# Pairs of experts in the first 16 blocks of a MoE layer: 4-byte matmuls in place of hi/lo parts, and one-hot matrices built a step ahead

## The chip, the core and the metric

The kernel runs on one core of a Trainium2 chip. The metric is device time of one launch in microseconds. The kernel before took 1333.95 us (median of 3 runs, 1331.36 to 1334.15).

## What is computed

One transformer layer over 512 latent and 256 context tokens (gated MLP with a tiny attention, neighbourhood attention, merge), then a mixture of 64 experts, 8 per token, and a shared expert. The change lies in the mixture and in the tables that route tokens to it. Cut to that:

```python
scores = sigmoid(h @ w_router)
_, idx = top_k(scores + b_router, 8)
wts = take(scores, idx) / sum * 2.5
# tokens are grouped by expert; each block holds rows of one expert
yb = (silu(h[tok] @ w_gate[e]) * (h[tok] @ w_up[e])) @ w_down[e] * wt
out[tok] += yb                       # for every expert e
```

The model width is 1024, an expert's inner width 256; everything is float32.

## The kernel before, in words

Up to some 600 us the kernel does the mixers, the router and the shared expert's first half. Then `experts` runs 50 blocks of 128 token rows. `ORDER` sets their order: four single experts (blocks 0 to 3), three pairs (4 to 6), two singles (7, 8), one extra block `x` (9) that takes the overflow rows of the experts of blocks 7 and 8 as a pair, then twelve times "pair, single, single", and four singles. A pair holds two experts of 64 rows each. Among the first 16 blocks there are six of length two: 4, 5, 6, 9, 10 and 13.

A block needs the experts' weights: per expert three tiles of 1 MB (two halves of gate and up, one of down), loaded by SP's queue into 13 slots (`pump`, `load_part`); a load is issued when a slot's last reader is done, and at most 4 (`DQ`) are under way. `drop` marks a slot free at its place in the program. The order of loads is: gate/up of the next block, then down of this one.

Tokens are gathered from DRAM by POOL (`fetch`, L1339), transposed on PE (`xpose`, L1351) and split by ACT and DVE into hi and lo parts of type fp32r (`split`, L99, L100). Weights are split the same way, by quarters of 128x1024 (`prep`): a cast on ACT (L1244) and a subtraction on DVE (L1246; on POOL for the quarters numbered in `PQ`). `prep` runs three quarters (`LQ`) ahead of the matmuls. `mm` (L1260) then multiplies: for a single six 128x512 matmuls a quarter. For a pair the stationary operand holds the hi tokens of one expert in one half and the lo tokens of the other in the other half, so that four matmuls a quarter and expert, 32 a block, give each product in two halves of PSUM, which `combine` (L1273 on ACT, L1274 on DVE) adds into an SBUF tile of the `y` buffers. `act` makes silu(gate)*up, `ph` transposes it, `py` (L1304) multiplies by the down weights, unsplit in 4-byte form (for a pair two 64-column matmuls side by side), scales, and scatters with add into one of two DRAM accumulators (L1326), in turn.

`tables` makes, in the background (`bg`, one piece after each quarter-step as long as fewer than `TBN` tables wait), the row lists of each block: a one-hot matrix `oh` on DVE, which compares slot numbers `iot` with the token's position `posm` (L1158 in an interleaved order of rows, L1163 for rows past the capacity), and small matmuls with `vals` (L1168). PE and SP follow the program's order there (`manual_schedule`); DVE, ACT and POOL are ordered by the scheduler. Six pieces of the shared expert's down product (three token blocks, two halves) are put in from block 5 on (`MS`), one a step.

Of the kernel before, what the change touches and what calls it, by code (L numbers as in the profile page):

```python
# [7 lines left out]
F32 = mybir.dt.float32  # L8
# [9 lines left out]
P = 128  # L18
# [51 lines left out]

def bcast(ap, n, off=0):
    return bass.AP(tensor=ap.tensor, offset=ap.offset + off, ap=[[0, P], [1, n]])


class Kern:
# [9 lines left out]
    SLOTS = [0, 1, 2, 3, 8, 9, 5, 7, 4, 6, 10, 11]  # L85

# [979 lines left out]
    def rank(self):  # L1066

        nc, mid, cst, tri, mb = self.nc, self.mid, self.cst, self.tri, self.mb
# [9 lines left out]
        nc.vector.tensor_tensor(krow, pc[:, :NE], cst[:, RC_A:RC_A + NE], op=ALU.mult)  # L1078
        nc.vector.tensor_tensor(krow, krow, cst[:, RC_C:RC_C + NE], op=ALU.add)
# [7 lines left out]
        nc.vector.tensor_scalar(self.perm, cst[:, RC_S:RC_S + P], sm[:, 2:3], None, op0=ALU.is_equal)  # L1087
        nc.tensor.matmul(po, lhsT=cst[:NE, RC_E:RC_E + P], rhs=self.perm[:NE, :NE], start=True, stop=True)
# [56 lines left out]
    def tables(self, blocks, posm, vals, ps=None):  # L1145
# [6 lines left out]
        for i, block in enumerate(blocks):  # L1152
            oh = pool.tile([P, 4, P], BF, name="oh", tag=tag, bufs=2)
            m = P // len(block)
            for p0, (r, t0, cap) in zip((0, m), block):

                k = cap // NQ
                nc.vector.tensor_tensor(oh[:, :, p0:p0 + cap].rearrange("p b (q i) -> p b q i", q=NQ),  # L1158
                                        self.iot[:, None, t0:t0 + cap].rearrange("p b (i q) -> p b q i", q=NQ)
                                        .to_broadcast([P, 4, NQ, k]),  # L1160
                                        posm[:, :, r:r + 1, None].to_broadcast([P, 4, NQ, k]), op=ALU.is_equal)
                if cap < m:
                    nc.vector.tensor_tensor(oh[:, :, p0 + cap:p0 + m],  # L1163
                                            self.iot[:, None, t0 + cap:t0 + m].to_broadcast([P, 4, m - cap]),
                                            posm[:, :, r:r + 1].to_broadcast([P, 4, m - cap]), op=ALU.is_equal)
# [4 lines left out]
            yield  # L1170
# [66 lines left out]
    def prep(self, st, i):  # L1237

        nc = self.nc
        j, q = st.parts[i]  # L1240
# [22 lines left out]
    def combine(self, st, i):  # L1263

        nc = self.nc
        j, q = st.parts[i]
        if st.n == 1 or q < 3:
# [11 lines left out]
    def act(self, st):  # L1279
        nc, p2 = self.nc, self.p2  # L1280
        pg = st.pg[0] if st.n == 1 else st.pgs
# [61 lines left out]
    def xpose(self, st, q):  # L1343
# [9 lines left out]
        self.split(hi, lo, tp.rearrange("p (k s t) -> p k s t", k=4, s=2))  # L1353

    def step(self, es=(), **kw):
        n = max(len(es), 1)
        st = SimpleNamespace(es=es, n=n, parts=[(j, q) for j in range(n) for q in range(4)], gq={}, pg={}, x=None, xg=None,
                             y=None, w=None, h=None, last=False, one=False, room=None, gu=[self.gu_of(e) for e in es], d=lambda i: self.raw[es[i], 2][1])
        st.__dict__.update(kw)
        for e in es:  # L1360
# [13 lines left out]
    def experts(self):  # L1374
# [9 lines left out]
        steps = [self.step([r for r, _, _ in block], block=block) for block in BLOCKS]  # L1384

        parts = lambda st, ns: [(e, n) for e in st.es for n in ns]
# [128 lines left out]
    def extra_block(self):  # L1515
# [10 lines left out]
        nc.vector.tensor_scalar(sm[:, 0, :], sm[:, 0, :], -4097.0, None, op0=ALU.add)  # L1526
        nc.vector.tensor_tensor(oh, self.iot[:, None, :P].to_broadcast([P, 4, P]),
# [14 lines left out]
        nc.vector.tensor_scalar(ex[:, 5:6], ex[:, 4:5], -4096.0, None, op0=ALU.add)  # L1542
        nc.vector.scalar_tensor_tensor(lt, self.iot[:, :NE], ex[:, 5:6], self.order, op0=ALU.is_equal, op1=ALU.mult,
# [60 lines left out]
def prep(inputs):  # L1604
# [61 lines left out]
    a["iota"] = np.broadcast_to(np.arange(2 * P, dtype=np.float32) - 4096, (P, 2 * P))  # L1666
    cst = np.zeros((P, RC_N), np.float32)
    cst[:, 0:12:3] = ar[:, None]
# [3 lines left out]
    cst[:, RC_A:RC_A + NE] = np.where(e < NS, 0, 64)  # L1672
    cst[:, RC_C:RC_C + NE] = np.where(e < NS, 1e6 - e, -e)
    cst[:, RC_K] = np.tile(cst[0, RC_A:RC_A + NE], 2)
    cst[:, RC_K + 1] = np.tile(cst[0, RC_C:RC_C + NE], 2)
    cst[:, RC_K + 2] = np.repeat([0, NE], NE)
    cst[:, RC_S:RC_S + P] = SEQ + [r + NE for r in SEQ]
    cst[:, RC_E:RC_E + P] = ar[:, None] % NE
# [3 lines left out]
    a["cst"] = cst  # L1682
# [27 lines left out]
```

## Time and profile before

| | |
|---|---|
| median of 3 runs | 1333.95 us |
| profiled execution | 1330.07 us, its span 1328.3 us |
| PE busy | 1199.6 us (90%) |
| DVE busy | 924.2 us (70%) |
| ACT busy | 666.6 us (50%) |
| POOL busy | 413.8 us (31%) |
| DMA | 353.36 MB, mean 266 GB/s |
| chain that ended last | DMA 25%, PE 10%, issue 9%, DVE 7% |

Busy times are of one profiled execution. PE's busy time counts matmuls whose ends are modelled and which overlap, so it is not a share of peak. The chain is followed back from the last instruction. The DMA share is the mean busy share of 16 DMA engines; it can read a little over 1.

### The profile page before, as it was taken

Reading aid. Unit: us, or ns where it says so; the run is one execution under the profiler, and the core shown is the slowest. Engines: PE = TensorE matmul, PEld = TensorE weight load, DVE = VectorE, ACT = ScalarE, POOL = GpSimd, SP = SyncE. Lnnn points to the kernel's source line nnn. Section 1 sums busy time; section 2 is a strip of 40 time slices with the busy share of each in tenths; the row PEclk is TensorE's granted clock in tenths of the full one; section 3 lists DMA queues with packets and bytes.
Section 4 is the critical chain, followed back from the end, with each engine's and each line's share of the span. In section 5 each row is a group of like instructions: output and inputs, shape, how many; then the busy total and the mean of one; then the engine's idle time right before and its main releaser. Section 6 shows DMA issues by size and latency. Waiting matters only on the chain.

```text
span 1328.3 us, 18642 instructions
## 1 busy us (share of the span) xinstructions
PE 1199.6 (90%) x6305; PEld 855.4 (64%) x6305; DVE 924.2 (70%) x1577; ACT 666.6 (50%) x1146; POOL 413.8 (31%) x379
## 2 busy tenths in 40 slices
PE   6999999999999999989787999899887997888991
PEld 4875887887777778876553555556554654655660
DVE  4535366666777767687997878877975976667763
ACT  4411254345655544335453666566564665656651
POOL 2410111701211100134554434444343433443422
PEclk9999999999999999989998999899998998999995
DMA  9999454944755546586789899999999999999994
GB/s 325 336 307 287 143 174 103 230 134 112 164 123 136 136 132 230 187 305 197 250 290 278 285 332 372 357 352 333 331 348 356 351 361 353 371 365 358 371 324 143
DMA packets 107322, 353.36 MB, mean 266 GB/s; under 512 B 13937, under 2 KB 41178, under 8 KB 82266
## 3 DMA queue, kind: packets, MB, share of 16 engines
q1 hardware_dynamic: 82634, 289.99, 61.7%
q0 software_dynamic: 24128, 60.59, 19.4%
q10 hardware_dynamic: 464, 1.59, 0.3%
q8 instruction: 50, 0.82, 0.2%
q14 instruction: 46, 0.38, 0.1%
HBM read 323.12 MB, written 39.53 MB: 273 GB/s over the span
## 4 chain that ended last, share of the span: by engine, by line
DMA 25%; PE 10%; issue 9%; DVE 7%; POOL 3%; ACT 1%; POOLq 0%; SPq 0%; DVEq 0%; ACTq 0%
DMA rw<-in_w_exp_dram 21%; PE py L1304 4%; PE pg L1260 4%; DVE gq L1246 3%; DMA accd<-y,ix 2%; DVE xx L100 1%; DMA xg<-h2d,half 1%; DVE oh L1158 1%; POOL xg L1339 1%; ACT gq L1244 1%; POOL accd L1326 1%; DMA accd<-y,half 1%; POOL accb L1326 1%; POOL y L1317 0%; PE xt L1351 0%
## 5 line engine op out<-in xcount | busy, mean ns | idle before, releaser
L1260 PE MATMUL pg<-gq,xx 128*128 128x512 f32 x1328 | 392.2, 432 | 0.6 <-DVE xx L100 0.5
L1246 DVE TENSOR_TENSOR gq<-rw,gq 128x1024 fp32r<-128x1024 f32 x258 | 326.7, 1278 | 75.2 <-ACT gq L1244 73.9
L1244 ACT CAST gq<-rw 128x1024 fp32r<-128x1024 f32 x264 | 272.9, 1047 | 81.1 <-PE pg L1260 48.5
L1260 PEld LDWEIGHTS pg<-gq,xx 128*128 128x128 f32 x1328 | 244.2, 195 | 90.2 <-issue 39.3
L1304 PE MATMUL py<-rw,hT 128*128 128x512 f32 (+1 forms) x560 | 213.3, 617 | 29.6 <-DMA rw<-in_w_exp_dram 28.4
L1317 POOL TENSOR_TENSOR y<-y,gf 128x512 f32<-128x512 f32 x52 | 84.6, 1626 | 283.7 <-ACT y L1316 283.6
L1304 PEld LDWEIGHTS py<-rw,hT 128*128 128x128 f32 (+1 forms) x560 | 73.7, 169 | 111.1 <-issue 98.8
L99 ACT CAST whi<-raw 128x1024 fp32r<-128x1024 f32 (+1 forms) x60 | 61.3, 1023 | 130.9 <-PE mmp L117 52.3
L100 DVE TENSOR_TENSOR wlo<-raw,whi 128x1024 fp32r<-128x1024 f32 (+1 forms) x60 | 71.3, 1189 | 75.8 <-ACT whi L99 75.8
L116 PE MATMUL mmp<-hhi,whi 128*128 128x512 f32 x256 | 103.8, 406 | 0.0
L118 PE MATMUL mmp<-hhi,wlo 128*128 128x512 f32 x256 | 101.1, 396 | 0.0
L117 PE MATMUL mmp<-hlo,whi 128*128 128x512 f32 x256 | 100.8, 394 | 0.0
L1339 POOL DMA_INDIRECT xg<-h2d,ix x50 | 59.0, 1180 | 82.8 <-PE xt L1351 50.5
L100 DVE TENSOR_TENSOR xx<-xt,xx 128x512 fp32r<-128x512 f32 x100 | 68.2, 684 | 15.5 <-ACT xx L99 15.1
L99 ACT CAST xx<-xt 128x512 fp32r<-128x512 f32 x100 | 58.3, 584 | 12.4 <-PE xt L1351 11.6
L771 POOL DMA_DIRECT2D q<-qdr x32 | 17.7, 554 | 147.9 <-PE stp L818 143.1
L1351 PE MATMUL xt<-ident,xg 128*128 128x128 f32 x400 | 60.7, 275 | 1.9 <-DMA xg<-h2d,half 1.9
L1326 POOL DMA_INDIRECT accb<-y,ix x31 | 56.0, 1806 | 11.1 <-POOL y L1317 7.4
L1351 PEld LDWEIGHTS xt<-ident,xg 128*128 128x128 f32 x400 | 49.5, 143 | 12.3 <-issue 2.7
L1319 DVE SCALAR_TENSOR_TENSOR y<-py,tw,gf 128x512 f32<-128x512 f32 x52 | 38.8, 745 | 26.0 <-PE py L1304 18.3
L116 PEld LDWEIGHTS mmp<-hhi,whi 128*128 128x128 f32 x256 | 48.2, 188 | 12.5 <-issue 3.0
L118 PEld LDWEIGHTS mmp<-hhi,wlo 128*128 128x128 f32 x256 | 48.1, 188 | 10.6 <-issue 0.8
(422 smaller groups left out, 2162.3 us busy)
## 6 DMA issues: line engine op xcount, KB each, us to landing
rw<-in_w_exp_dram SPq DMA_DIRECT2D x195, 1024.0 KB
raw<-in_w_in_dram SPq DMA_DIRECT2D x40, 512.0 KB
araw<-in_w_ada_dram SPq DMA_DIRECT2D x64, 256.0 KB
araw<-in_w_ada_dram SPq DMA_DIRECT2D x16, 512.0 KB
k<-kdr POOLq DMA_DIRECT2D x32, 192.0 KB, 6.3
nab<-in_nab_dram SPq DMA_DIRECT2D x24, 256.0 KB
x<-in_x_dram SPq DMA_DIRECT2D x8, 512.0 KB
q<-qdr POOLq DMA_DIRECT2D x32, 128.0 KB, 5.1
```

The lines of the kernel that those rows point to most:

```text
L99: self.nc.scalar.copy(hi, src)
L100: (eng or self.nc.vector).tensor_tensor(lo, src, self.r32(hi), op=ALU.subtract)
L116: mm(ps, lhsT=ahi, rhs=bhi, start=first, stop=False)
L117: mm(ps, lhsT=ahi, rhs=blo, start=False, stop=False)
L118: mm(ps, lhsT=alo, rhs=bhi, start=False, stop=last)
L1244: nc.scalar.copy(t[:, 0, :, sl], src)
L1246: eng.tensor_tensor(t[:, 1, :, sl], src, self.r32(t[:, 0, :, sl]), op=ALU.subtract)
L1260: nc.tensor.matmul(pg, lhsT=st.x[:, q * 2 + k, a, :], rhs=t[:, b, k, :], start=q + k + n == 0, stop=q + k + n == 3 + len(terms))
L1304: nc.tensor.matmul(py[s], lhsT=st.hT[:, j, s], rhs=d[:, j * D + c * 512:j * D + c * 512 + 512], start=j == 0, stop=j == 1)
L1317: nc.gpsimd.tensor_tensor(o, o, gf, op=ALU.mult)
L1326: nc.gpsimd.indirect_dma_start(out=to[:], out_offset=bass.IndirectOffsetOnAxis(ap=ix[:cap], axis=0), in_=y, in_offset=None, bounds_check=S ...
L1351: self.nc.tensor.transpose(tp[:, k * P:k * P + P], st.xg[:, (q * 4 + k) * P:(q * 4 + k + 1) * P], self.ident)
```

## The change

For the six blocks of length two among the first `NB` = 16 (`whole`), tokens and weights are not split. `xpose` copies the transposed tokens as they are; `prep` only looks the tiles up; `mm` multiplies 4-byte tokens of each expert (64 columns) with the weight tile itself, the two experts side by side in the halves of PSUM. Such a block has 4 steps of two experts' quarters instead of 8 of one. Its gate/up tiles are dropped after the matmuls that read them, both experts' first halves together, and are loaded in that order. `combine` does nothing and `act` reads PSUM.

In the tables the slot numbers are kept in bfloat16, in the interleaved order already (`SLOTS_OF`, 896 columns, cast by a POOL DMA), so that one comparison without strides makes each expert's part; `posm` gets one more instruction. The `yield` moves up: a block's `oh` is made in one step and its table matmuls run in the next. The constants for `rank` move to a tile of their own in the `u` buffers.

```diff
+    NB = 16
 def place(...):
         nc.vector.scalar_tensor_tensor(posm, mask, -4096.0, pp, op0=ALU.mult, op1=ALU.add)
+        nc.vector.tensor_scalar(posm, posm, 4096.0, None, op0=ALU.add)
 def route_consts(self):
-        self.iot = mid.tile([P, 2 * P], F32, name="iot")
-        nc.sync.dma_start(self.iot, self.A["iota"])
+        self.iot = mid.tile([P, len(SLOTS_OF)], BF, name="iot")
+        nc.gpsimd.dma_start(self.iot, self.A["iota"])
...
+        self.cst2 = self.p1.tile([P, RK_N], F32, name="cst2", tag="u", bufs=2)
+        nc.sync.dma_start(self.cst2, self.A["cst2"])
 def tables(...):
-                k = cap // NQ
-                nc.vector.tensor_tensor(oh[:, :, p0:p0 + cap].rearrange("p b (q i) -> p b q i", q=NQ),
...
-                if cap < m:
...
+                c = TURNS[m, t0, cap]
+                nc.vector.tensor_tensor(oh[:, :, p0:p0 + m], self.iot[:, None, c:c + m].to_broadcast([P, 4, m]),
+                                        posm[:, :, r:r + 1].to_broadcast([P, 4, m]), op=ALU.is_equal)
+
+            yield
             for b in range(4):
...
-            yield
 def prep(self, st, i):
+        if st.whole:
+            q = st.parts[i]
+            st.gq[i] = [st.gu[j](q)[0][0] for j in range(st.n)]
+            return
 def mm(self, st, i):
+        if st.whole:
+            q, m = st.parts[i], P // st.n
+            if q == 0:
+                st.pg[0] = self.ps2.tile([P, 512], F32, name="pg", tag="gu", bufs=2)
+            for k in range(2):
+                for j, t in enumerate(st.gq[i]):
+                    r = slice(j * m, j * m + m)
+                    nc.tensor.matmul(st.pg[0][r], lhsT=self.r32(st.x)[:, q * 2 + k, 0, r], rhs=t[:, k, :],
+                                     start=q + k == 0, stop=q + k == 4)
+            if q % 2:
+                for e in st.es:
+                    self.drop(e, q // 2)
+            return
 def combine(self, st, i):
+        if st.n == 1 or st.whole:
+            return
 def xpose(self, st, q):
-        self.split(hi, lo, tp.rearrange("p (k s t) -> p k s t", k=4, s=2))
+        if st.whole:
+            self.nc.scalar.copy(self.r32(st.x)[:, q * 4:q * 4 + 4, 0, :], tp.rearrange("p (k t) -> p k t", k=4))
+        else:
+            self.split(hi, lo, tp.rearrange("p (k s t) -> p k s t", k=4, s=2))
 def experts(self):
+        steps = [self.step([r for r, _, _ in block], block=block, whole=len(block) > 1 and i < self.NB)
+                 for i, block in enumerate(BLOCKS)]
+        parts = lambda st, ns: [(e, n) for n in ns for e in st.es] if st.whole else [(e, n) for e in st.es for n in ns]
```

On PE, in the second step of block 5 (a pair), the order before was this (`pg` the gate/up product, `xt` the transposed tokens of the next block, `ph` the transposed inner rows and `py` the down product of the block before or of the shared expert, `ptab` a table):

```order
L1260 MATMUL pg<-gq,xx 128x512 x4
L1290 MATMUL ph<-ident,hh 128x128 x2
L1304 MATMUL py<-rw,hT 128x512 x2
L1168 LDWEIGHTS oh
L1168 MATMUL ptab<-vals,oh 128x6
```

And the same step now:

```order
L1281 MATMUL pg<-rw,xx 64x512 x4
L1326 MATMUL ph<-ident,hh 128x128 x2
L1387 MATMUL xt<-ident,xg 128x128 x4
L1340 MATMUL py<-rw,hT 128x512 x2
L1186 LDWEIGHTS oh
L1186 MATMUL ptab<-vals,oh 128x6
```

The step's `pg` covers a quarter of both experts instead of one, so a block has half as many steps, and the next block's transposes come in the first half of the block.

On DVE, the stretch between two blocks' down products inside the pairs read as follows before (`gq` the lo part of a weight quarter, `y<-y,pg` the sum of the halves, `hh` the inner rows):

```order
L1319 SCALAR_TENSOR_TENSOR y<-py,tw,gf 128x512
L1158 TENSOR_TENSOR oh<-iot,posm_6304 128x4x64 x2
L1158 TENSOR_TENSOR oh<-iot,posm_6304 128x512
L1274 TENSOR_TENSOR y<-y,pg 64x512
L1246 TENSOR_TENSOR gq<-rw,gq 128x1024
L1158 TENSOR_TENSOR oh<-iot,posm_6304 128x512
L1158 TENSOR_TENSOR oh<-iot,posm_6304 128x4x64 x2
L1246 TENSOR_TENSOR gq<-rw,gq 128x1024
L100 TENSOR_TENSOR xx<-xt,xx 128x4x128 x2
L1246 TENSOR_TENSOR gq<-rw,gq 128x1024
```

And now:

```order
L1355 SCALAR_TENSOR_TENSOR y<-py,tw,gf 128x512
L1180 TENSOR_TENSOR oh<-iot,posm_6307 128x4x64 x2
L1321 TENSOR_TENSOR hh<-sg,pg 128x256
L1180 TENSOR_TENSOR oh<-iot,posm_6307 128x512
L1350 TENSOR_TENSOR y<-py,gf 128x512
L1180 TENSOR_TENSOR oh<-iot,posm_6307 128x512
L1180 TENSOR_TENSOR oh<-iot,posm_6307 128x4x64 x2
L1355 SCALAR_TENSOR_TENSOR y<-py,tw,gf 128x512
```

The weight and token subtractions and the sums of halves are gone there; one-hot matrices and the output products remain.

## Rows read from the trace of the kernel before

**Rows 1.** The timeline of PE: first gate/up matmuls of block 4 and of block 7.

```profile
672.84 1.18 PE L1260 MATMUL pg<-gq,xx 128*128 128x512 f32 x4
...
746.73 1.64 PE L1260 MATMUL pg<-gq,xx 128*128 128x512 f32 x6
```

**Rows 2.** Stages (from:to, us): PE, PEld, DVE, ACT, POOL busy; PEclk, DMA share, GB/s.

```profile
618.00:672.00 54.00, 45.99 (x241) 32.29 (x240) 52.43 (x80) 27.47 (x42) 34.16 (x19) 0.94 0.77 242
672.00:747.00 75.00, 62.02 (x284) 35.66 (x283) 65.85 (x92) 37.35 (x49) 32.56 (x19) 0.86 0.95 296
747.00:820.00 73.00, 66.99 (x283) 41.61 (x283) 56.52 (x64) 47.95 (x67) 32.33 (x23) 0.98 0.96 328
820.00:950.00 130.00, 119.34 (x561) 76.98 (x560) 107.53 (x151) 82.23 (x112) 59.77 (x38) 0.97 1.01 347
950.00:1250.00 300.00, 258.88 (x1106) 167.29 (x1105) 215.73 (x247) 179.28 (x247) 120.03 (x81) 0.97 1.02 357
```

**Rows 3.** DMA from 618, 672, 820 us: bytes; a queue's share; scatters, us to landing.

```profile
DMA packets 2546, 13.09 MB, mean 242 GB/s; under 512 B 640, under 2 KB 640, under 8 KB 1261
...
DMA packets 3775, 22.21 MB, mean 296 GB/s; under 512 B 595, under 2 KB 595, under 8 KB 1537
q0 software_dynamic: 1267, 3.86, 26.1%
...
accd<-y,rows POOLq DMA_INDIRECT x2, 9.4
...
DMA packets 26096, 152.29 MB, mean 354 GB/s; under 512 B 4827, under 2 KB 4827, under 8 KB 10219
```

**Rows 4.** The chain that ended last, in order of time: start, us, what.

```profile
735.49 1.87 PE py L1304 x8
737.36 1.14 PE pg L1260 x4
...
763.07 1.72 PE py L1304 x4
...
773.17 0.92 PE pg L1260 x4
```

**Rows 5.** Groups of instructions, shapes apart: xcount | busy us, mean ns | idle before.

```profile
L1260 PE MATMUL pg<-gq,xx 128*128 128x512 f32 x1328 | 392.2, 432 | 0.6 <-DVE xx L100 0.5
L1246 DVE TENSOR_TENSOR gq<-rw,gq 128x1024 fp32r<-128x1024 f32 x258 | 326.7, 1278 | 75.2 <-ACT gq L1244 73.9
L100 DVE TENSOR_TENSOR xx<-xt,xx 128x512 fp32r<-128x512 f32 x100 | 68.2, 684 | 15.5 <-ACT xx L99 15.1
L1274 DVE TENSOR_TENSOR y<-y,pg 64x512 f32<-64x512 f32 x32 | 21.9, 684 | 14.6 <-ACT y L1273 14.1
L1158 DVE TENSOR_TENSOR oh<-iot,posm 128x512 bf16<-128x512 f32 x13 | 13.2, 1024 | 0.0
L1158 DVE TENSOR_TENSOR oh<-iot,posm 128x256 bf16<-128x256 f32 x16 | 12.6, 817 | 0.0
L1057 DVE SCALAR_TENSOR_TENSOR posm<-sw,pp 128x256 f32<-128x256 f32 x1 | 0.4, 401 | 0.0
```

**Rows 6.** Busy time of instructions on tile oh alone: PE, PEld, DVE, PEclk, DMA share, GB/s.

```profile
618.00:672.00 54.00, 2.86 (x52) 2.18 (x52) 14.22 (x16) 0.94 0.77 242
672.00:747.00 75.00, 4.42 (x80) 3.62 (x80) 22.30 (x31) 0.86 0.95 296
```

**Rows 7.** Timeline of DVE and of POOL: single instructions.

```profile
657.46 0.28 DVE L1158 TENSOR_TENSOR oh<-iot,posm 128x128 bf16<-128x128 f32 x1
...
555.60 0.56 POOL L121 TENSOR_TENSOR sm<-sm,mhalf 128x1 f32<-128x1 f32 x1 [62.41 <-DVE sm L955]
```

**Rows 8.** Waits: of the stage 672 to 747 us, and of the whole span.

```profile
ACT y L1273 <- DMA accd<-y,rows: 7.4, 1, 7.4
ACT y L1316 <- DMA accd<-y,half: 6.9, 1, 6.9
...
PE py L1304 <- DMA rw<-in_w_exp_dram: 28.4, 7, 7.0
```

More of the change, by code (lines that the diff above doesn't have):

```diff
@@ L68, with turns @@
 BLOCKS, SEQ = plan(ORDER)
+def turns():
+    runs, at = [range(NE)], {}
+    n = NE
+    for block in BLOCKS:
+        m = P // len(block)
+        for _, t0, cap in block:
+            if (m, t0, cap) not in at:
+                at[m, t0, cap] = n
+                n += m
+                runs.append([t0 + (p % (cap // NQ) * NQ + p // (cap // NQ) if p < cap else p) for p in range(m)])
+    return at, [t for r in runs for t in r]
+TURNS, SLOTS_OF = turns()
 def bcast(ap, n, off=0):
@@ L1066, in rank @@
     def rank(self):
-        nc, mid, cst, tri, mb = self.nc, self.mid, self.cst, self.tri, self.mb
+        nc, mid, cst, cst2, tri, mb = self.nc, self.mid, self.cst, self.cst2, self.tri, self.mb
         col = lambda i: cst[:, i:i + 1]
@@ L1077, in rank @@
         krow = mid.tile([P, NE], F32, name="krow")
-        nc.vector.tensor_tensor(krow, pc[:, :NE], cst[:, RC_A:RC_A + NE], op=ALU.mult)
-        nc.vector.tensor_tensor(krow, krow, cst[:, RC_C:RC_C + NE], op=ALU.add)
+        nc.vector.tensor_tensor(krow, pc[:, :NE], cst2[:, RK_A:RK_A + NE], op=ALU.mult)
+        nc.vector.tensor_tensor(krow, krow, cst2[:, RK_C:RK_C + NE], op=ALU.add)
         sm = mid.tile([P, 4], F32, name="rsm")
@@ L1086, in rank @@
         self.perm = mid.tile([P, P], F32, name="perm")
-        nc.vector.tensor_scalar(self.perm, cst[:, RC_S:RC_S + P], sm[:, 2:3], None, op0=ALU.is_equal)
-        nc.tensor.matmul(po, lhsT=cst[:NE, RC_E:RC_E + P], rhs=self.perm[:NE, :NE], start=True, stop=True)
+        nc.vector.tensor_scalar(self.perm, cst2[:, RK_S:RK_S + P], sm[:, 2:3], None, op0=ALU.is_equal)
+        nc.tensor.matmul(po, lhsT=cst2[:NE, RK_E:RK_E + P], rhs=self.perm[:NE, :NE], start=True, stop=True)
         self.order = mid.tile([P, NE], F32, name="order")
@@ L1280, in act @@
         nc, p2 = self.nc, self.p2
-        pg = st.pg[0] if st.n == 1 else st.pgs
+        pg = st.pg[0] if st.n == 1 or st.whole else st.pgs
         sg = p2.tile([P, FF], F32, name="sg", tag="sg", bufs=1)
@@ L1358, in step @@
                              y=None, w=None, h=None, last=False, one=False, room=None, gu=[self.gu_of(e) for e in es], d=lambda i: self.raw[es[i], 2][1])
+        st.whole = False
         st.__dict__.update(kw)
+        if st.whole:
+            st.parts = list(range(4))
         for e in es:
@@ L1525, in extra_block @@
         oh = p2.tile([P, 4, P], BF, name="xoh", tag="oh", bufs=2)
-        nc.vector.tensor_scalar(sm[:, 0, :], sm[:, 0, :], -4097.0, None, op0=ALU.add)
-        nc.vector.tensor_tensor(oh, self.iot[:, None, :P].to_broadcast([P, 4, P]),
+        nc.vector.tensor_scalar(sm[:, 0, :], sm[:, 0, :], -1.0, None, op0=ALU.add)
+        c = TURNS[P, 0, P]
+        nc.vector.tensor_tensor(oh, self.iot[:, None, c:c + P].to_broadcast([P, 4, P]),
                                 sm[:, 0, :, None].to_broadcast([P, 4, P]), op=ALU.is_equal)
@@ L1665, in prep @@
     a["tri"] = np.stack([ar[:, None] < ar[None], np.ones((P, P), bool)], 1).astype(np.float32)
-    a["iota"] = np.broadcast_to(np.arange(2 * P, dtype=np.float32) - 4096, (P, 2 * P))
+    a["iota"] = np.broadcast_to(np.array(SLOTS_OF, np.float32), (P, len(SLOTS_OF)))
     cst = np.zeros((P, RC_N), np.float32)
+    cst2 = np.zeros((P, RK_N), np.float32)
     cst[:, 0:12:3] = ar[:, None]
@@ L1671, in prep @@
     e = np.arange(NE)
[L1672 to L1675, printed above, removed]
+    cst2[:, RK_A:RK_A + NE] = np.where(e < NS, 0, 64)
+    cst2[:, RK_C:RK_C + NE] = np.where(e < NS, 1e6 - e, -e)
+    cst[:, RC_K] = np.tile(cst2[0, RK_A:RK_A + NE], 2)
+    cst[:, RC_K + 1] = np.tile(cst2[0, RK_C:RK_C + NE], 2)
     cst[:, RC_K + 2] = np.repeat([0, NE], NE)
-    cst[:, RC_S:RC_S + P] = SEQ + [r + NE for r in SEQ]
-    cst[:, RC_E:RC_E + P] = ar[:, None] % NE
+    cst2[:, RK_S:RK_S + P] = SEQ + [r + NE for r in SEQ]
+    cst2[:, RK_E:RK_E + P] = ar[:, None] % NE
     for block in BLOCKS:
@@ L1681, in prep @@
             cst[:, RC_L + r] = max(cst[0, RC_L + r], t0 + cap)
-    a["cst"] = cst
+    a["cst"], a["cst2"] = cst, cst2
     return {k: np.ascontiguousarray(v) for k, v in a.items()}
```

18 lines of the change are left out of this document (4 added, 14 removed).

## The prediction

> **What bounds the kernel now.** I read the busy times by stage first, then the DMA figures of the stages, the chain, the groups, and the waits. In PE's timeline block 4's first matmul starts at 672.84 us and block 7's at 746.73 [rows 1], which cuts the expert part into stages: A, 618 to 672 us, blocks 0 to 3; B, 672 to 747, the three pairs 4 to 6; C, 747 to 820; and the rest. The reader should look at which column is nearly full in each row of [rows 2].
>
> In A, DVE is busy for 52.4 of 54 us and the DMA for a share of 0.77 only: weight loads wait for slots, and slots for DVE. In B, DVE has 65.9 of 75 us, PE 62.0 at a granted clock of 0.86 of 2.4 GHz (part of the time at 1.2), and the DMA 0.95. In C, PE has 67.0 of 73 us, the DMA 0.96. From 820 us on the DMA stands at 1.01 to 1.02 for 430 us. PE waits for weights there, 28.4 us in all for the down product [rows 8]. So three limits follow each other: DVE, then PE, then the DMA; and whatever the first two lose is lost for good only as far as the DMA idles. The DMA is the bank: once it is full, time gained ahead of it comes through to the end only as DMA work that was done earlier.
>
> I take 1.02, the late stages' share, as full. The DMA work in A, B and C is 54 x 0.77 + 75 x 0.95 + 73 x 0.96 = 41.6 + 71.3 + 70.1 = 183.0 us of share, which takes 179.4 us at 1.02, in place of 202. The most that can be gained by this reckoning is 22.6 us: 13.2 in A, 9.4 in B and C.
>
> **PE.** A pair's 32 gate/up matmuls go in fours of 0.92 us [rows 4], 7.4 us a block. Now there are 16 matmuls of 64 columns, 4-byte, with the experts side by side. The trace has this form already in a pair's down product: eight records, which are four matmuls, in 1.87 us, where a single's four records (two matmuls of 128 columns) take 1.72 [rows 4]. Two halves therefore run together, and 16 matmuls take 4 x 1.87 = 7.5 us: even. One thing is added: four full-width matmuls right behind a 64-column `py` take 1.14 us against 0.92 [rows 4], so a return from half width costs 0.22 us. A whole block returns to full width once a step, 0.9 us a block. The Trainium skill (TensorEngine Tiling (Array Packing), Key Properties) says that changing the tiling mode drains the engine, which speaks against this change; it gives no time, so the sum by the page would only say "more than 7.5", and the row's 0.22 us stands.
>
> **DVE, stage A.** The one-hot instructions there take 14.2 us in 16 records [rows 6]. After the change the same blocks (five pairs, four singles) need 14 comparisons without strides. Such an instruction isn't in the trace; the token subtraction, one pass over 512 elements, takes 684 ns [rows 5]. It can't be slower than today's strided one (1024 ns [rows 5]), and the 128-element one of 0.28 us [rows 7], less than a third of which would be its start, gives about 0.4 us for 512 at the very least. I take 684, which is nearest in form, and 0.41 for 256 elements (between 0.28 and today's 0.82): 4 x 0.68 + 10 x 0.41 = 6.8, so 7.4 us saved (0 to 9). Block 4's first three quarters are prepared in A, one on POOL and two on DVE, 2 x 1.28 = 2.6 us [rows 5]; two token subtractions of 0.68 make 1.4 us. The added instruction on `posm` costs what its neighbour does, 0.4 us [rows 5], and is on the way to the first table. DVE falls by 11.0 to 41.4 us. PE is late next, with 46.0 us busy; of the 8.0 us in which it stands still I keep half, for the making of the first routing tables, which the change leaves as they are. Stage A: 50 instead of 54, **4 us** gained.
>
> **DVE, stage B.** The 24 - 3 = 21 weight subtractions x 1.28 are 26.9 us, six sums of halves x 0.68 4.1, four token subtractions 2.7, and half of the tables' steps go: 22.3 us of one-hot work [rows 6] becomes some 8. DVE falls from 65.9 to 17.9 us. PE is next: its 62.0 us at a clock of 0.86 are 53.3 at full clock; 2.6 come for returns, and half of the tables' 4.4 us [rows 6] goes, 53.7 us of 75. The scatters come close: block 3's one, three shared ones and two each of blocks 4 and 5 go into two accumulators in turn, landing in 9.4 us [rows 3], so five in a row take some 47 us. The stall that they make today through the `y` buffers, 7.4 and 6.9 us on ACT [rows 8], should shrink, since a whole block takes no `y` tile for its sums. So engines could do B in 54 us, and C, with two whole blocks' returns, in 69.
>
> **DMA.** It can't follow that: 141.4 us of share work in B and C need 138.6 us at 1.02, more than the engines' 123. B and C thus take 138.6 in place of 148: **9.4 us** gained. Behind 820 us nothing changes but the start.
>
> **Sum.** 4 + 9.4 = 13.4 us. The profiled execution took 1330.07 us (span 1328.3), 3.9 below the median of 1333.95. 1330.1 - 13.4 = 1316.7 there, 1320.5 as a median; I say 1320.
>
> **What costs nothing, and its cover.** The `iot` load goes to POOL's queue, behind `tri` and ahead of the first `sm`; POOL stands idle for 62.4 us there [rows 7]. Were the cover gone it would be one issue, which I put at the 0.56 us of its neighbour there [rows 7]. On SP `cst2` takes one `u` buffer and the router's weights the next, one `nab` load later; only the loads queued behind could suffer, by the time until the second buffer is free, and three raw buffers stand between them and PE. ACT loses eight casts a pair, which nobody waits for once DVE is out of the way. One POOL subtraction moves from block 4 to block 7.
>
> **The wait that is added.** A slot of a whole block now waits for PE's matmul instead of DVE's subtraction, which ran up to three quarters ahead: on average half a block later. On SP all later loads and the reads of expert numbers queue behind. Against that, when block 4 starts, 6 of 13 slots are held (a shared tile, block 3's down, its own four); the seven others take all of block 5's gate/up, block 4's down and one of block 6. That is a block ahead, with four loads allowed at once, so I cost it at nothing.
>
> **Rivals.**
>
> *Bytes, not shares* (chance 0.22). A share of 0.95 in B moves 296 GB/s, the same core moves 354 in the late stages [rows 2, 3]. If the difference is hidden idling and not the indirect transfers (26.1% of share in B for 3.86 of 22.21 MB [rows 3], which speaks for these), B and C with 46.2 MB need 130 us at 354, a gain of 17.6, with A 21.6: 1312, and to 1305 if A too gets fuller. The Trainium skill (DMA: Bandwidth & Descriptors, Specifications) puts the HBM limit of a core at about 358 GB/s; by it B and C would need 129 us, the same rival. The trace agrees with it: 357 over 300 us [rows 2].
>
> *Slots held too long: slower* (0.14). If the later drop starves the loads, B and C run nearer to A's manner. With 0.90 in B and C they need 141.4/0.90 = 157 us, 9 more than now, less A's 4: 1339. At A's own 0.77 it would be 184 us and the kernel past 1360, which the seven free slots make unlikely. The point that decides is a share of 0.93 over B and C, where A's gain is used up. The row for it is A's 0.77, made by slots.
>
> *No change* (0.13). The halves don't run together when weights are the moving operand and tokens the stationary one, so that the change doesn't do what it says on PE: 16 matmuls x 0.86 = 13.8 us a block instead of 7.5. B then needs 73 us on PE, C (blocks 9 and 10) 81, together 154 against 148, which eats A's 4 us and 2 more: 1336. Against it stands the identical form of `py`. Or the indirect transfers keep their time whatever comes, and only 2 us are won.
>
> **Numbers.** The forecast has 0.51, with 1313 to 1329 as its own range. A measurement can tell about 0.2%, 2.7 us, from no change. Faster by more, below 1331.3: 0.51 + 0.22 = 0.73; within: 0.13; slower: 0.14. The range leaves out the outer part of the bytes rival and most of the slower one: 1306 to 1335.
>
> **What would show it.** On DVE 258 weight subtractions become some 210 and 32 sums of halves 20; 1328 fp32r gate/up matmuls become 1136, with 192 records of the 4-byte form, eight in 1.87 us. One-hot instructions on DVE are 34 + 2 x 16 = 66, a 512-element one near 0.68 us. Block 7's first matmul should come 20 to 28 us earlier if the engines alone decide, and PE should wait for weights from about there, much earlier than now; the DMA share from 670 us on at 1.0 or above. I am wrong in the sum if block 7 starts early but the last weights don't land some 13 us earlier; wrong in the mechanism if the share in B falls below 0.93, or if eight 4-byte records take over 3 us.

## The result, and the profile after

The changed kernel takes 1315.93 us (median of 4 runs, 1313.55 to 1321.14) where the kernel before takes 1334.05 in the same comparison (4 runs, 1331.36 to 1335.59): a ratio of 0.988, 95% interval 0.9856 to 0.9905, 18.1 us less. The profiled execution of the change took 1315.69 us with a span of 1313.8, so the two profiled spans differ by 14.5. That is less than 18.1 because the profiled execution of the kernel before, at 1330.07 us, was 3.9 faster than its median.

PE's timeline, which answers to [rows 1]: the first gate/up matmul of all, of block 4 and of block 7.

```profile
622.54 1.96 PE L1294 MATMUL pg<-gq,xx 128*128 128x512 f32 x6
...
671.50 1.94 PE L1281 MATMUL pg<-rw,xx 128*64 128x512 f32 x8
...
721.65 1.66 PE L1294 MATMUL pg<-gq,xx 128*128 128x512 f32 x6
```

Block 7 starts 25.1 us earlier. Stage A, counted from the first gate/up matmul, now lasts 49.0 us and stage B 50.2, where [rows 1] and the first gate/up matmul at 618.2 give 54.7 and 73.9. The stages again, cut at the new borders, in the columns of [rows 2]:

```profile
618.00:671.00 53.00, 48.68 (x254) 33.52 (x255) 47.12 (x81) 28.18 (x45) 31.88 (x19) 0.97 0.78 246
671.00:721.00 50.00, 49.24 (x246) 18.74 (x245) 18.51 (x34) 13.20 (x22) 21.14 (x15) 1.00 0.98 346
721.00:806.00 85.00, 79.61 (x366) 40.68 (x362) 40.71 (x54) 33.27 (x50) 40.55 (x32) 0.96 1.00 346
806.00:936.00 130.00, 110.98 (x514) 68.73 (x513) 88.83 (x112) 69.63 (x96) 50.28 (x34) 0.93 1.00 341
936.00:1236.00 300.00, 263.62 (x1114) 169.78 (x1113) 214.63 (x247) 182.12 (x251) 121.89 (x84) 0.96 1.02 361
```

In stage B, DVE fell to 18.5 us, PE is busy for 49.2 of 50 at full clock, and the DMA moves 346 GB/s instead of 296. From 671 us on the DMA is as good as full (0.98 and 1.00, where 1.0 or above was forecast), and the engines begin to wait for it: not PE first, as forecast, but ACT's cast, which stands ahead of PE. From 671 to 806 us (in all, times, longest) it waited for weights

```profile
ACT gq L1265 <- DMA rw<-in_w_exp_dram: 13.9, 6, 6.4
```

where the kernel before had 1.3 us of that wait. The groups, columns as in [rows 5]:

```profile
L1294 PE MATMUL pg<-gq,xx 128*128 128x512 f32 x1136 | 331.6, 428 | 0.8 <-DVE gq L1267 0.8
L1267 DVE TENSOR_TENSOR gq<-rw,gq 128x1024 fp32r<-128x1024 f32 x210 | 264.1, 1270 | 82.5 <-ACT gq L1265 81.4 <-issue 0.3
L1281 PE MATMUL pg<-rw,xx 128*64 128x512 f32 x192 | 48.1, 623 | 0.0
L1180 DVE TENSOR_TENSOR oh<-iot,posm 128x512 bf16<-128x512 bf16 x34 | 26.2, 774 | 10.0 <-PE ptab L1186 8.5 <-PE ph L1326 1.4
L1180 DVE TENSOR_TENSOR oh<-iot,posm 128x256 bf16<-128x256 bf16 x32 | 17.5, 578 | 5.8 <-PE ptab L1186 5.8
L1310 DVE TENSOR_TENSOR y<-y,pg 64x512 f32<-64x512 f32 x20 | 13.7, 685 | 9.6 <-ACT y L1309 9.3
```

The counts are those forecast (210, 20, 1136, 192, 34 and 32). An undisturbed 512-element one-hot takes 0.68 to 0.69 us; the mean of 774 ns holds a few that took much longer.

Where the time went is read best from the DMA's bytes between 618 and 820 us. Ahead of 618 the program is nearly the same, and behind 820 the DMA is full in both. First the kernel before, then the change (all traffic; then the weights' queue with its share):

```profile
DMA packets 10671, 59.26 MB, mean 293 GB/s; under 512 B 2111, under 2 KB 2111, under 8 KB 4778
...
q1 hardware_dynamic: 6605, 48.16, 65.5%
```

```profile
DMA packets 11729, 64.33 MB, mean 318 GB/s; under 512 B 2347, under 2 KB 2347, under 8 KB 5422
...
q1 hardware_dynamic: 7072, 51.56, 66.6%
```

The change moves 5.07 MB more in this window, and 5.07 MB at the 354 GB/s of [rows 3] are 14.3 us: the spans differ by 14.5. The weights' share rose by a mere 1.1 points of 202 us, 2.2 us of share, for 3.4 MB more. With POOL's queue, which went from 24.6% to 27.1%, it is 3.6 points or 7.3 us, half of what came. This is the main reading of the case: bytes tell what was banked, the share doesn't.

### The profile page after: what moved, and what is told of

It is laid out like the page before. It is cut to its first block, busy times and chain, and to the rows that moved or that the text cites. A ratio compares the mean times of both kernels' runs of the same rounds, so it can differ in the third digit from the quotient of the medians.

```text
span 1313.8 us, 18428 instructions
## 1 busy us (share of the span) xinstructions
PE 1199.2 (91%) x6305; PEld 835.5 (64%) x6305; DVE 831.2 (63%) x1470; ACT 612.5 (47%) x1086; POOL 397.7 (30%) x380
## 4 chain that ended last, share of the span: by engine, by line
DMA 30%; PE 15%; DVE 5%; issue 3%; ACT 1%; POOL 1%; SPq 0%; POOLq 0%; DVEq 0%; ACTq 0%
DMA rw<-in_w_exp_dram 27%; PE py L1340 5%; PE pg L1294 5%; DVE gq L1267 2%; PE pg L1281 2%; PE xt L1387 1%; DMA accb<-y,rows 1%; DMA xg<-h2d,half 1%; DMA accd<-y,ix 1%; DVE oh L1180 1%; PE mmp L137 1%; DMA accb<-y,ix 1%; ACT gq L1265 1%; PE mmp L136 1%; PE mmp L135 1%
## 5 line engine op out<-in xcount | busy, mean ns | idle before, releaser
L1294 PE MATMUL pg<-gq,xx 128*128 128x512 f32 x1136 | 331.6, 428 | 0.8 <-DVE gq L1267 0.8
L1267 DVE TENSOR_TENSOR gq<-rw,gq 128x1024 fp32r<-128x1024 f32 x210 | 264.1, 1270 | 82.5 <-ACT gq L1265 81.4
L1294 PEld LDWEIGHTS pg<-gq,xx 128*128 128x128 f32 x1136 | 207.0, 192 | 78.7 <-issue 30.2
L1265 ACT CAST gq<-rw 128x1024 fp32r<-128x1024 f32 x216 | 222.0, 1047 | 64.7 <-DMA rw<-in_w_exp_dram 42.1
L1340 PE MATMUL py<-rw,hT 128*128 128x512 f32 (+1 forms) x560 | 216.9, 625 | 37.2 <-DMA rw<-in_w_exp_dram 30.0
L1353 POOL TENSOR_TENSOR y<-y,gf 128x512 f32<-128x512 f32 x52 | 75.1, 1445 | 270.6 <-ACT y L1352 270.5
L119 DVE TENSOR_TENSOR xx<-xt,xx 128x512 fp32r<-128x512 f32 x88 | 60.2, 685 | 30.4 <-ACT xx L118 29.7
L1375 POOL DMA_INDIRECT xg<-h2d,ix x50 | 55.4, 1107 | 76.8 <-PE xt L1387 45.7
L1387 PEld LDWEIGHTS xt<-ident,xg 128*128 128x128 f32 x400 | 49.2, 143 | 20.6 <-issue 13.2
L118 ACT CAST xx<-xt 128x512 fp32r<-128x512 f32 x88 | 51.4, 585 | 16.3 <-PE xt L1387 15.4
```

Of the source, the lines that this page charges most:

```text
L118: self.nc.scalar.copy(hi, src)
L119: (eng or self.nc.vector).tensor_tensor(lo, src, self.r32(hi), op=ALU.subtract)
L1265: nc.scalar.copy(t[:, 0, :, sl], src)
L1267: eng.tensor_tensor(t[:, 1, :, sl], src, self.r32(t[:, 0, :, sl]), op=ALU.subtract)
L1294: nc.tensor.matmul(pg, lhsT=st.x[:, q * 2 + k, a, :], rhs=t[:, b, k, :], start=q + k + n == 0, stop=q + k + n == 3 + len(terms))
L1340: nc.tensor.matmul(py[s], lhsT=st.hT[:, j, s], rhs=d[:, j * D + c * 512:j * D + c * 512 + 512], start=j == 0, stop=j == 1)
```

## Experiments

All are compared with runs of the kernel before on the same chip (ratio and its 95% interval). The table has one profiled execution of each: first gate/up matmul, length of stage A (to block 4's first matmul) and B (to block 7's), from PE's timeline; MB moved from 618 to 820 us; the span; and what the bytes alone would give, 1328.3 - (MB - 59.26)/0.354.

| kernel | ratio | start | A | B | MB | span | by bytes |
|---|---|---|---|---|---|---|---|
| before | 1 | 618.2 | 54.7 | 73.9 | 59.26 | 1328.3 | |
| change | 0.988 (0.9856 to 0.9905) | 622.5 | 49.0 | 50.2 | 64.33 | 1313.8 | 1314.0 |
| change again | 0.988 (0.9847 to 0.9912) | 618.3 | 49.0 | 49.1 | 65.74 | 1309.6 | 1310.0 |
| tables only | 0.9948 (0.9923 to 0.9972) | 622.5 | 53.9 | 70.2 | 59.30 | 1328.1 | 1328.2 |
| 4-byte pairs only | 0.9893 (0.9853 to 0.9933) | 616.9 | 54.4 | 49.0 | 64.37 | 1317.1 | 1313.9 |
| blocks 4 to 6 | 0.9846 (0.9809 to 0.9883) | 619.0 | 49.0 | 49.3 | 66.83 | 1312.0 | 1306.9 |
| all pairs | 0.9813 (0.9777 to 0.9849) | 619.8 | 49.4 | 49.9 | 65.17 | 1308.6 | 1311.6 |
| all pairs again | 0.9843 (0.9812 to 0.9874) | 617.1 | 53.1 | 49.1 | 64.68 | 1309.3 | 1313.0 |
| all but block 9 | 0.9833 (0.9794 to 0.9873) | 622.7 | 53.1 | 50.2 | 63.50 | 1314.1 | 1316.3 |
| halves in turn | 0.9864 (0.9821 to 0.9907) | 620.4 | 53.3 | 49.6 | 63.59 | 1318.9 | 1316.1 |
| work put back | 0.9915 (0.9885 to 0.9945) | 618.9 | 54.0 | 49.1 | 63.29 | 1317.3 | 1316.9 |
| sums in own tile | 0.9913 (0.9885 to 0.9942) | 617.8 | 53.3 | 63.2 | 63.61 | 1319.9 | 1316.0 |
| one half | one run | 618.3 | 49.4 | 50.5 | 65.06 | 1312.5 | 1311.9 |
| same step | 0.9897 (0.9866 to 0.9928) | 621.1 | 51.2 | 49.0 | 64.34 | 1317.9 | 1313.9 |

The last two columns agree within 5.1 us over the 13 profiles, whatever was edited, and for eight of them within 3.0. Reckoned by the DMA's share of the same window instead (all queues, 1.02 as full), all 13 would end later than they do, by 2.4 to 12.3 us.

What the bytes leave over is hardly noise alone. The three kernels with the late pairs in 4-byte form (all pairs twice, all but block 9) end 2.2 to 3.7 us before what the bytes give; of the ten others none ends more than 0.4 us before. Behind 820 us these three move 340.0 to 340.8 GB/s to their end, the others 334.8 to 339.0. So the stretch behind 820 us is not quite the same in every kernel.

**1. The two parts apart.** Tables only: no pair in 4-byte form.

```diff
-    NB = 16
+    NB = 0
```

> The changed kernel with no pair in 4-byte form: one-hot tables without strides, made a step ahead, all else as before. Bank theory (time won ahead of the DMA-bound part comes through as DMA work done earlier): stage A ends some 4 us earlier, and in the pairs the one-hot work falls by 8 to 10 us of a DVE that had 65.9 of 75 us, of which a third to a half counts; in all 4 to 8 us, 1326 to 1330 us. Tables-do-most rival: 14 us or more, 1320 or less. No-value rival (late start again, DVE's time taken by the next wait): within 2.7 us of 1334.

4-byte pairs only: the kernel before with the change's edits to `prep`, `mm`, `combine`, `act`, `xpose`, `step` and the order of loads, and the tables, `iota` and `cst` as they were. Against the changed kernel that is, in the tables:

```diff
-                c = TURNS[m, t0, cap]
-                nc.vector.tensor_tensor(oh[:, :, p0:p0 + m], self.iot[:, None, c:c + m].to_broadcast([P, 4, m]),
-                                        posm[:, :, r:r + 1].to_broadcast([P, 4, m]), op=ALU.is_equal)
-            yield
+                k = cap // NQ
+                nc.vector.tensor_tensor(oh[:, :, p0:p0 + cap].rearrange("p b (q i) -> p b q i", q=NQ),
...
```

> The kernel before with pairs among the first 16 blocks in 4-byte form; one-hot tables with strides and not a step ahead, as before. Bank theory: stage A as before, B shorter by some 20 us on the engines, of which 10 to 14 us reach the end: 1320 to 1324 us. Tables-do-most rival: 1329 or more. If the two parts of the change add, the gains of this kernel and of the tables alone sum to about 18 us; if each alone is enough to fill the DMA queue, their sum is well over 18.

Measured: 1327.88 us and 1320.02 us against 1335.61, so 7.7 and 15.6 less. The sum, 23.3, is over the 18.1 of both, but the intervals (some 3 and 5 us to either side) don't exclude that they add. The 4-byte pairs carry the larger part, and all of the shortening of B (49.0). The tables alone take 3.7 us out of B. Their profiled execution shows nothing of the 7.7 us: it starts at 622.5 us, its A takes 53.9, and its span of 1328.1 is that of the kernel before, so that gain rests on the medians alone. In B the next wait grew in place of the one-hot work; ACT's waits from 672 to 747 us of the tables-only kernel:

```profile
ACT y L1309 <- DMA accd<-y,rows: 12.3, 1, 12.3
```

It was 7.4 us before [rows 8]. The copy that waited starts at 712.78 us, and ACT's next cast of a weight only behind it, at 713.26.

**2. Sums of halves in a tile of their own**, in the tables-only kernel, to test that wait.

```diff
-            st.y = self.y_tile()
-            st.pgs = st.y[:, 512:]
+            st.pgs = self.p2.tile([P, 512], F32, name="pgs", tag="pgs", bufs=1)
...
-        st.h = p2.tile([P, FF], F32, name="hh", tag="hh", bufs=2)
+        st.h = p2.tile([P, FF], F32, name="hh", tag="hh", bufs=1)
```

> The tables alone (no pair in 4-byte form), and the sums of halves in a tile of their own instead of a y buffer, so that no scatter holds them up; hh has one buffer to make room. y-buffer theory (in stage B a two-part pair's sum waits for an earlier scatter, 7.4 us before and 12.3 us with the tables alone, and ACT's casts queue behind it): stage B falls from 74 to 60 to 66 us, and the kernel, 7 us faster with the tables alone, gains 4 to 8 us more: 1319 to 1324 us. Chain rival (what costs is cast, subtraction and product in turn, wherever the sum stands): B stays above 70 us, and the kernel is that of the tables alone, 1325 to 1329.

Measured: 1322.11 us against 1333.12, and B 63.2 us, as the y-buffer theory had it. Its stage B, from block 4 to block 7, and block 7's first matmul:

```profile
671.00:734.00 63.00, 57.15 (x282) 32.57 (x281) 55.90 (x78) 36.51 (x48) 32.14 (x18) 0.95 0.97 333
```

```profile
734.27 1.64 PE L1294 MATMUL pg<-gq,xx 128*128 128x512 f32 x6
```

PE has 57 and DVE 56 of the 63 us, so with the wait gone both are near full. B's 23.7 us thus go by steps: 3.7 by the tables, 7.0 by not waiting for a `y` buffer, and the last 13 only when the pairs need no split (one profile of each). At the end, the ratio goes from 0.9948 to 0.9913; the intervals overlap a little.

**3. The weights' split put back**, without a reader.

```diff
             st.gq[i] = [st.gu[j](q)[0][0] for j in range(st.n)]
+            for src in st.gq[i]:
+                t = self.p2.tile([P, 2, 2, 2 * FF], F32R, name="gq", tag=f"gq{self.ngq % self.GQ}")
+                self.ngq += 1
+                nc.scalar.copy(t[:, 0], src)
+                eng = nc.gpsimd if self.ngq in self.PQ else nc.vector
+                eng.tensor_tensor(t[:, 1], src, self.r32(t[:, 0]), op=ALU.subtract)
             return
```

> The changed kernel with the weight casts (ACT) and subtractions (DVE, POOL) of the 4-byte pairs put back into tiles that nobody reads; sums of halves and token subtractions stay away, tables and PE stay as changed. DVE theory: the 21 subtractions of 1.28 us in stage B bring DVE back to some 45 us and, in turn with ACT's casts, hold slots and the SBUF; if DVE's relief is the gain, stage B returns to 60 to 70 us and the kernel to 1322 to 1328. PE rival (the gain of B is the half-as-many PE steps and PE's clock): B stays near 50 us and the time near 1316. On the DMA: if the weights' bytes per unit of share fall from 391 GB/s towards before's 357 with DVE busy again, the engines' traffic is what made the DMA slower in B; if they stay near 390, the queue's depth is.

Measured: 1321.69 us against 1331.34, between the two forecasts. Its stage B:

```profile
673.00:722.00 49.00, 49.00 (x251) 18.75 (x249) 44.94 (x56) 28.83 (x39) 24.69 (x14) 1.00 0.96 344
```

DVE is busy for 44.9 of 49 us again, and B is no longer for it. So DVE's load alone is not what made B slow. In experiment 2, where the split is still there, PE is busy for 57.2 of 63 us at a clock of 0.95; here it is busy for all 49.0 at 1.00. So of the last 13 us some 6 are waits of PE, which went with its dependence on cast, subtraction and sum, and the rest is PE's own work, which is less in the 4-byte form and at a higher clock. How much is the clock and how much the work, no run took apart. From 671 to 721 us the weights' queue moved 13.80 MB in a share of 0.693, 398 GB/s of share; the 391 of the change did not fall, so DVE's traffic is not what made the DMA slower before. Against the change on the same chip (1316.14 us, experiment 7) the kernel is 5.5 us slower, so the work isn't free. A took 54.0 us in its profile, the longer of two lengths that other kernels show as well, so whether the extra work cost that time is open.

**4. Do two 64-column halves run together?** First the loops swapped, so that one expert's two matmuls of a quarter come before the other's.

```diff
-            for k in range(2):
-                for j, t in enumerate(st.gq[i]):
+            for j, t in enumerate(st.gq[i]):
+                for k in range(2):
```

> The changed kernel with the two loops around the 4-byte matmul swapped, so that one expert's two matmuls of a quarter come before the other's. Pairing theory (two halves of the array run together only when neighbours in the order stand on different halves): eight records take 2.6 to 3.4 us instead of 1.87 to 1.94, a pair's gate/up 10 to 14 us instead of 7.5 to 8, stage B some 8 to 18 us longer on PE, and 5 to 15 us of that reach the end: 1320 to 1331. If the halves run together in whichever order, 1314 to 1318.

Then one half left alone.

```diff
                 for j, t in enumerate(st.gq[i]):
+                    if j and q + k not in (0, 4):
+                        continue
```

> The changed kernel, in which the second expert of a 4-byte pair leaves out its gate/up product except the first and the last of its eight matmuls; so the two middle quarters have two matmuls of 64 columns (four records) with no neighbour on the other half. Half-price theory (a 64-column 4-byte matmul takes half of a 128-column one by itself): four records in 0.9 to 1.0 us. Pairing theory (two halves run at the same time): four records alone take as long as eight together, 1.7 to 1.9 us.

Measured: swapped, 1314.89 us against 1331.34, B 49.6; eight records still take 1.94 us. A quarter of the swapped kernel, then block 4's second quarter of the kernel with one half alone:

```profile
676.24 1.94 PE L1281 MATMUL pg<-rw,xx 128*64 128x512 f32 x8
678.12 0.44 PE L1326 MATMUL ph<-ident,hh 128*128 128x128 f32 x2
```

```profile
673.01 1.91 PE L1283 MATMUL pg<-rw,xx 128*64 128x512 f32 x4
674.85 1.55 PE L1342 MATMUL py<-rw,hT 128*128 128x512 f32 x3
```

Four records of one half alone, with the next instruction 1.84 us behind, take as long as eight of both: the halves do run at the same time, and a half alone gains nothing. But they need not take turns in the program; the expectation of 2.6 to 3.4 us for the swapped order fell. The Trainium skill (TensorEngine Tiling (Array Packing), Key Properties) says that different tiles of the array can load weights and multiply in parallel, of which the four records bear out the multiplying; of the order it says nothing.

**5. How many pairs.** `NB = 7` (blocks 4 to 6), `NB = 50` (every pair) twice, and every pair but block 9:

```diff
-        steps = [self.step([r for r, _, _ in block], block=block, whole=len(block) > 1 and i < self.NB)
+        steps = [self.step([r for r, _, _ in block], block=block, whole=len(block) > 1 and i < self.NB and i != 9)
```

> The changed kernel with only blocks 4 to 6 in 4-byte form; the pairs 9, 10 and 13 back in two parts. Bank theory: the DMA is full from 721 us on, so the engines' extra work there is hidden: 1314 to 1319 us, the same as the change. Slots rival (a 4-byte pair holds its slots for longer, as in the gap in the weight loads from 735 to 755 us): without blocks 9, 10 and 13 in that form 3 to 8 us faster, 1308 to 1313. If instead the engines still bound that stretch: 4 to 10 us slower, 1320 to 1326.

> The changed kernel with every pair in 4-byte form, ten more behind block 16. Bank theory: the DMA is full there whatever the engines do, so 1313 to 1319 us, the same as the change. Slots rival: each added pair holds its slots later and lets the DMA share fall below 1.0 behind block 16: slower than 1320. Engine rival (PE and DVE still cost time between 806 and 1236 us): faster, 1305 to 1312.

> Every pair in 4-byte form, once more. If its 1309.8 us were more than a good draw: again 1307 to 1312 us and a ratio of 0.979 to 0.984, below the 0.988 that the change gave twice. If the late pairs are hidden by the DMA, as the bank theory has it: 1313 to 1317 and 0.986 to 0.990.

> Every pair in 4-byte form except block 9 (the two experts' overflow), which goes back to two parts. Slots theory: block 9's four tiles, held until PE has read them, made the gap in the weight loads from 735 to 755 us; without it the weights lead by some 27 us instead of 14 at the 49th load, and the kernel is 2 to 5 us faster than with all pairs in that form: 1304 to 1308 us. Bank theory by bytes: the DMA share is 0.98 there either way, an earlier weight only comes in place of a gather or a scatter, and the time is that of all pairs, 1308 to 1312. If block 9's two-part form costs more on DVE than it gives: above 1313.

Measured: 1313.55 and 1309.80 against 1335.61; all pairs again 1312.45 against 1333.12; all but block 9 1312.26 against 1331.34. Block 9 does make a hole. From 735 to 755 us, in the change and then without block 9 in 4-byte form:

```profile
735.00:755.00 20.00, 14.61 (x54) 7.26 (x52) 8.10 (x16) 7.09 (x10) 11.57 (x9) 0.87 0.95 291
```

```profile
735.00:755.00 20.00, 19.72 (x81) 12.18 (x81) 18.30 (x29) 11.62 (x16) 12.49 (x9) 1.00 1.03 338
```

By SP's timeline the 49th weight load is then issued 20.2 us ahead of before instead of 10.0, with a start as late; but at the 70th the lead is 8.0 against 10.6, and the end is no better: 1312.26 us misses the 1304 to 1308 of the slots theory. Blocks 4 to 6 alone, at 1313.55, fall between the two first expectations.

Every pair in 4-byte form has the lowest ratio measured, 0.981, and 0.984 the second time. Both medians lie below the 1313 us from which the bank theory starts, the first inside the 1305 to 1312 of the engine rival. On one chip the six runs with all pairs took 1308.1 to 1311.7 us where the six with blocks 4 to 6 alone took 1311.8 to 1317.5, some 4 us between the medians, though the intervals of the ratios overlap. With what the bytes leave over under the table this speaks against the later pairs' form being hidden by the DMA altogether. Against the change, with 0.988 twice, all pairs look some 5 us better by the ratios, but the profiled spans (1308.6 and 1309.3) are within 1 us of the change's second (1309.6); the two were never compared on one chip, and how much is gained over the change stays open.

**6. One-hot in the same step as its product**, as before.

```diff
-            yield
             for b in range(4):
                 for p0, (r, _, _) in zip((0, m), block):
...
                                      start=b == 0, stop=b == 3)
+            yield
```

> The changed kernel with the one-hot matrix made in the same step as its product, as before. If the step ahead matters: PE waits for DVE's one-hot again (8.1 us in stage B of the kernel before), 3 to 8 us of stages A and B are lost and the kernel is at 1318 to 1324 us. If it doesn't, because a comparison of 0.4 to 0.7 us on an idle DVE is made in time anyway: 1313 to 1318.

Measured: 1318.66 us against 1333.12; the interval overlaps the change's. PE does wait again, though in A and not in B: from 618 to 672 us its weight loads waited 7.1 us for the one-hot, against 1.6 in either profile of the change's A. A takes 51.2 us, B 49.0. Stages A and B together are 100.1 us, against 99.1 and 98.1 in the two profiles of the change. That the step ahead is worth anything at the end isn't shown.

**7. The change once more.**

> The changed kernel itself, beside the other three on one chip. If the half clock between 590 and 597 us and the first gate/up matmul 4.4 us late belong to this order of instructions, both come again and the time is 1314 to 1318 us; if they are chance of an execution, the profile may start at 618 to 620 us and the time is 1310 to 1316.

Measured: 1316.14 us against 1331.34. The profiled execution starts at 618.25 us, and its span is 1309.6. In the first profile of the change, PE's granted clock was 0.53 from 590 to 600 us, most of it at the lower level of 1.2 GHz; in the second it was 1.00. Ten microseconds a row, the first profile and then the second:

```profile
580.00:590.00 10.00, 8.01 (x44) 6.44 (x42) 7.69 (x21) 3.55 (x9) 2.58 (x5) 0.84 0.97 367
590.00:600.00 10.00, 10.00 (x41) 8.21 (x41) 5.34 (x20) 3.69 (x7) 2.48 (x4) 0.53 0.51 212
```

```profile
580.00:590.00 10.00, 7.76 (x45) 6.16 (x45) 7.69 (x21) 3.79 (x10) 2.58 (x5) 0.92 0.92 338
590.00:600.00 10.00, 9.97 (x71) 7.98 (x72) 9.17 (x38) 4.16 (x8) 2.53 (x4) 1.00 0.58 241
```

In the ten microseconds ahead, PE was busy for 8.0 and for 7.8 of 10 us, so the fall isn't told from that. What goes with the late start is the clock itself: the four profiles of the table with 0.50 to 0.72 in that row start at 620.4 to 622.5 us, and of the ten with 1.00 nine start at 616.9 to 619.8; the tenth (all but block 9, 622.7) had its 0.66 in the row ahead. So the late start isn't the change's own, and between its two profiles it comes through to the end: 4.3 us of start, 4.2 of span.

## Why the prediction was right, and where it was not

The forecast was 1320 us (1306 to 1335), the measurement is 1315.93; 18.1 us were gained where 13.4 to 14 were forecast.

**The three limits and the bank: right.** B shortened by 24 us and the end came 14.5 us earlier (profiled) because the DMA took over. The 4.3 us of start, lost ahead of the DMA-bound part, came through between the two profiles, and the bytes moved by 820 us give the end within 5.1 us. What the bank theory leaves out is the stretch behind 820 us, where the form of the late pairs, which the change leaves alone, seems to count too (experiment 5).

**The term that was mis-sized: DMA, 9.4 us for B and C.** The step was "141.4 us of share work in B and C need 138.6 us at 1.02". It took a share for a fixed amount of work. It isn't: from 618 to 820 us the weights' queue moved 48.16 MB in 0.655 x 202 us of share before, 364 GB/s of share, and 51.56 in 0.666 x 202, 383, after. From 672 to 820 us the change moved 51.12 MB (26.30 up to 747 us and 24.82 behind) where the kernel before moved 46.17; 4.95 MB at 354 GB/s are 14.0 us. In A it moved 13.21 MB against 13.09, 0.3 us: the late start took up what A had gained. In the second profile it is 14.5 us in B and C and 3.8 in A. The rival *Bytes, not shares* named this; by its own sum of 1312 it was 4 us too low, as the forecast was 4 too high, since B and C reached 345 GB/s and not 354. Why a unit of share carries more is open: it isn't DVE's traffic (experiment 3), nor the 4-byte form, since it rose to 381 GB/s in the kernel of experiment 2, which has no such pair. The Trainium skill's limit of about 358 GB/s for a core (DMA: Bandwidth & Descriptors, Specifications), cited with the rival, is passed a little by the 361 GB/s that the change reaches over 300 us, and far by single slices (last section).

**A, 4 us: about right by chance.** A fell to 49.0 to 49.4 us in five of the profiles with the new tables, but stayed at 53 to 54 in six others and took 51.2 in one. The step on DVE failed: 41.4 us were forecast, 44.4 measured between the first gate/up matmul and block 4's (47.1 in the row above, which counts from 618 us). A single one-hot cost what was forecast, 0.68 and 0.41, but the 14 in A took 9.2 us together, not 6.8: three of them took 0.7 to 1.1 us over their kind, each beside an instruction of POOL (last section), a cost that the sum puts at nothing. From 0.41 us for 256 elements and 0.68 for 512, the fixed part of one is some 0.14 us by estimate; that is half of the 0.28 us of which the forecast, for its lower bound, took less than a third. PE is busy for 45.0 of the 49.0 us, so DVE is neither well out of the way, as forecast, nor the only limit. The two lengths go with the same thing: in each of the six long A's one DVE instruction, 37 to 42 us into the stage, takes 1.6 to 3.5 us over its kind beside POOL; in the five short ones none there takes over 0.9 more. Why POOL's instruction falls there in one kernel and not in the other wasn't traced.

**B, DVE 17.9 us: right, PE 53.7: 4.5 too high.** Measured were 18.5 and 49.2; which part of PE's sum was too large wasn't taken apart. The 7.5 us of a pair's gate/up are 4 x 1.87, from one quarter to what follows it, and the halves do run together. The return from half width shows once more in the chain of the change, by which four `py` records right behind the 64-column group take 1.92 us, and behind transposes the 1.72 of [rows 4]:

```profile
678.76 1.92 PE py L1340 x4
...
687.07 1.72 PE py L1340 x4
```

That is 0.20 us as against the 0.22 taken. What the forecast did not price is the order in which B's causes come off: DVE's work (tables) first gave 3.7 us, since the wait for `y` buffers, called a stall that "should shrink", was worth 7.0.

**What was costed at nothing: right within what can be measured.** The second profile of the change starts at 618.25 us against 618.18, so `iota`, `cst2` and the late router weights cost nothing that the start shows. The added wait for slots shows as a hole around block 9; with that block in two parts the hole is gone, but neither the lead at the 70th load nor the end is better. *Slots held too long* fell with a share of 0.98 to 1.00 in B and C, *No change* with the four records that take as long as eight.

## What to carry to other kernels

Where a DMA-bound stretch follows, count in bytes moved by its start, not in busy share: here the bytes moved up to 820 us gave the end in 13 profiles within 5.1 us, while the share left out 2.4 to 12.3. A wait that names an old scatter on one engine can be the limit of a stage in which no engine is full; take it away alone before paying for a new form of the work. Put removed work back without a reader: if the stage doesn't mind, that engine's load alone was not the cost. And where one DVE instruction takes several times its kind, look at what POOL does beside it.

## What was not expected

- The DMA moves far more in single slices than in any stage. Stage B of the change in 40 slices of 1.25 us:

```profile
GB/s 157 174 374 328 138 197 324 423 406 406 357 318 380 400 406 419 410 312 298 374 400 423 426 315 256 252 344 439 426 426 419 419 419 354 203 265 354 321 338 426
```

Slices of 419 to 439 stand beside slices of 138 to 260, though nearly all of them are 90% busy or more. So the 361 GB/s of the best stage is no ceiling for a slice here, and why a stage's mean stays at 340 to 361 was not taken apart.
- DVE instructions beside elementwise instructions of POOL can take several times their kind. One subtraction of 64 elements (`xt` from `xend` and `xc`, L1540) took 3.13 us in 11 of 11 profiles with the one-hot made a step ahead, and 0.22 without (before, 4-byte pairs only, same step). In the 11 a weight subtraction of POOL runs beside it, in the other three no instruction of POOL does. DVE, then POOL, from the second profile of the change:

```profile
650.88 3.13 DVE L1540 TENSOR_TENSOR xt__11797<-xend,xc 128x64 f32<-128x64 f32 x1
...
651.53 2.39 POOL L1267 TENSOR_TENSOR gq<-rw,gq 128x1024 fp32r<-128x1024 f32 x1
```

- Other single DVE instructions in A take 1 to 2 us more than their kind, at places that change from run to run. The same weight subtraction in the second profile of the change, with nothing but POOL's issue of a DMA beside it, and in the kernel with the loops swapped, with POOL's sum of a product beside it, and what PE then waited for in the latter:

```profile
654.60 1.20 DVE L1267 TENSOR_TENSOR gq<-rw,gq 128x1024 fp32r<-128x1024 f32 x1
```

```profile
658.16 2.82 DVE L1267 TENSOR_TENSOR gq<-rw,gq 128x1024 fp32r<-128x1024 f32 x1
...
658.62 1.27 POOL L1353 TENSOR_TENSOR y<-y,gf 128x512 f32<-128x512 f32 x1
...
662.03 0.71 PE L1186 MATMUL ptab<-vals,oh 128*64 128x6 bf16 x8 [4.16 <-DVE oh L1180]
```

Over all 14 profiles, among the forms that occur eight times or more in one, 234 DVE instructions take over 0.5 us more than the median of their form. Every one of them overlaps an elementwise instruction of POOL; of the 14962 that overlap none, not one is so slow. But 1216 others overlap one too and are not, and no run moved POOL's work away, so which overlaps cost is open.
